# Order of the first modulation sum on VectorE, and of two side loads on the sync queue, in a hybrid decoder layer

## The chip, the core and the metric

The kernel runs on one core of a Trainium2 chip. The metric is the device time of one execution in microseconds, the median of several executions; smaller is better. Engines are named as in the profile: PE is TensorE (PEld its weight loads), DVE is VectorE, ACT is ScalarE, POOL is GpSimd, SP is the sync engine, whose queue (SPq) issues most DMAs; ACT issues some too (ACTq).

## What is computed

One decoder layer over 512 tokens of width 1024 (batch 1, depth 1). The change touches only the start: the modulation vector, the first norm, and the first projection.

```python
cond = jax.nn.silu(c)
mod = cond @ ada_w[l] + ada_b[l]
sh1, sc1, g1, sh2, sc2, g2 = jnp.split(mod[:, None, :], N_MOD, axis=-1)

u = rms_norm(x, mix_pre_g[l]) * (1.0 + sc1) + sh1
proj = u @ w_in[l]
...
x = x + g1 * rms_norm(mix, mix_post_g[l])
...
x = x + g2 * rms_norm(f, ffn_post_g[l])
```

Behind `proj` come a four-head mLSTM, a causal convolution of width 31 with a layer norm, the output projection, and a gated convolutional feed-forward block. All matrix products of the projections are made with operands that are split into a high and a low part (three matmuls for one).

## The kernel before

Channels lie on the 128 partitions for most of the kernel: the 1024 channels are `KT` = 8 blocks of 128, the 512 tokens are 4 tiles (`NT`).

**Opening.** `x` is loaded token by token (`xn`, eight pieces of 256 KB). For each of the four token tiles ScalarE and VectorE sum the squares of half the row each (L256, L257), VectorE adds them (`xs`, L265), GpSimd raises the sum to the power -1/2 (L266), and `x_turn` (L238 on) multiplies the identity with that factor on VectorE (`dg`, L240) and lets TensorE multiply `xn` with `dg` (L242): that turns the first four channel blocks of the tile and applies the norm in one go. A fifth matmul spreads the factor over the partitions (`rb`, L243). The other four blocks (`xr4` to `xr7`) are loaded already turned from a second input, `xT`, and are multiplied with `rb` later (L354).

**Modulation.** `cb` holds silu(c), spread over all partitions. `ada_sum(k, i)` (L271) is one VectorE instruction over 128x1024 elements: a piece of the modulation matrix (`ada`, 512 KB, loaded by `first_load`, L220) times `cb`, summed along the row, into a column of `part[k]`. Two such sums give scale and shift of channel block `k`; L334 and L335 make `gs` and `sh` (tile `gsk`) of them.

**The first projection** is a loop over the eight blocks `k` (L317). Each turn loads a weight block `wglu0` (512 KB, two buffers), splits it on ScalarE (L170, L324) and VectorE (L171, L339), makes the high part `uh` of the block's input on ScalarE (L341, L358, L361) and the low part `ul` on VectorE (L344, L365, L367), makes the two sums of block k + 1, and runs 24 matmuls of 128x512 into eight accumulators (L316, later L188 to L190). Each turn also issues side loads on SP: the two `ada` pieces of block k + 1 or later (two buffers, so the load waits for the sums that free one), one block of `xT` in turns 1 to 4 (L331), and in turn 1 the rest of the vectors (`vec[:, FIRST:]`, 296 KB, L328), whose first reader is L408 behind the loop.

**Order.** Within the opening `in_order` keeps VectorE, ScalarE and GpSimd in the order in which the code is written. A DMA is issued when all ahead of it on its queue are, and when its buffer is free. Behind the opening a scheduler sets the order of each engine from a plan of its own, so an edit in the opening can also exchange neighbours far behind it. There the convolution's taps (L731, 200 instructions on VectorE) fill the time between the instructions on which TensorE waits.

Of the kernel before, what the change touches and what calls it, by code (L numbers as in the profile page):

```python
# [10 lines left out]
F32 = mybir.dt.float32  # L11
F32R = mybir.dt.float32r
BF16 = mybir.dt.bfloat16
AF = mybir.ActivationFunctionType
ALU = mybir.AluOpType
PSUM = bass.MemoryType.PSUM

P = 128
D = 1024
# [33 lines left out]
def decoder_layer(ctx, tc, w_glu0, x, xT, c, adaT, vecs, w_glu, w_qko, w_v0, w_v, w_out, w_up, w_down, out):  # L53
    nc = tc.nc
    V, S, G, PE = nc.vector, nc.scalar, nc.gpsimd, nc.tensor
# [10 lines left out]
    small = ctx.enter_context(tc.tile_pool(name="small", bufs=6))  # L66
# [17 lines left out]
    def slot(name, dt=F32):  # L84
        return slots.tile([P, T], dt, tag="t", name=name)

    def mmbank(name):
        return psum.tile([P, T], F32, tag="mm", bufs=4, name=name)

    def atbank(name):  # L90
        return psum.tile([P, T], F32, tag="at", bufs=2, name=name)
# [27 lines left out]
    cb = const.tile([P, D], F32, name="cb")  # L119
# [9 lines left out]
    def vcol(name, i):  # L129
        a = VEC[name][0] + i  # L130
        return vec[:, a : a + 1]

    def vcols(name, i, n):
        a = VEC[name][0] + i
        return vec[:, a : a + n]
# [28 lines left out]
    def w_split(src, name, pool=None, tag="w", eng=None):  # L164

        n = src.shape[1]
        pool = pool or wpool
        hi = pool.tile([P, T], F32R, tag=tag, name=f"{name}h")
        lo = pool.tile([P, T], F32R, tag=tag, name=f"{name}l")
        S.activation(hi[:, :n], src, AF.Copy)  # L170
        (eng or G).tensor_tensor(out=lo[:, :n], in0=src, in1=hi[:, :n].bitcast(F32), op=ALU.subtract)  # L171
        return hi, lo
# [46 lines left out]
    first = []  # L219

    def first_load(k):

        r = raws.tile([P, 2048], F32, tag="raw", name=f"ada{k}")
        for i in range(2):
            nc.sync.dma_start(r[:, i * D : (i + 1) * D], adaT[k][:, i * D : (i + 1) * D])
        first.append(r)
# [8 lines left out]
    TURNED = KT // 2  # L235

    def x_turn(tt, xs):

        dg = slot(f"dg{tt}")[:, :P]
        V.tensor_scalar(out=dg, in0=ident, scalar1=xs[:, 1:], scalar2=None, op0=ALU.mult)  # L240
        for j in range(TURNED):
            PE.matmul(xT_ps[j][:, tt * P : (tt + 1) * P], xn[tt][j // NT][:, j % NT * P : (j % NT + 1) * P], dg, start=True, stop=True)  # L242
        PE.matmul(rb_ps[:, tt * P : (tt + 1) * P], ones, dg, start=True, stop=True)  # L243

    xT_ps = [mmbank(f"xT{j}") for j in range(TURNED)]
    rb_ps = atbank("rb")
    last = None
    for tt in range(NT):
        if tt == 2:
            bp1 = const.tile([P, KT], F32, name="bp1")  # L250
            V.tensor_scalar(out=bp1, in0=vcols("ada_b", 0, 2 * KT).rearrange("p (j two) -> p j two", two=2)[:, :, 0], scalar1=1.0, scalar2=None,
                            op0=ALU.add)
            g32 = const.tile([P, KT], F32, name="g32")
            V.tensor_scalar(out=g32, in0=vcols("mix_pre_g", 0, KT), scalar1=RD, scalar2=None, op0=ALU.mult)
        xsq = small.tile([P, 2], F32, tag="adap", name=f"xsq{tt}")
        S.activation(xjunks[0], xn[tt][0], AF.Square, accum_out=xsq[:, :1])  # L256
        V.scalar_tensor_tensor(out=xjunks[1], in0=xn[tt][1], scalar=1.0, in1=xn[tt][1], op0=ALU.mult, op1=ALU.mult, accum_out=xsq[:, 1:])  # L257
        if tt == 1:
            S.activation(cb, cps, AF.Silu)
            cspool.__exit__(None, None, None)  # L260
            cvpool.append(ctx.enter_context(tc.tile_pool(name="cvpool", bufs=2, space=PSUM)))
        if tt:
            x_turn(tt - 1, last)
        last = small.tile([P, 2], F32, tag="gsk", name=f"xs{tt}")
        V.tensor_scalar(out=last[:, :1], in0=xsq[:, :1], scalar1=xsq[:, 1:], scalar2=D * EPS, op0=ALU.add, op1=ALU.add)  # L265
        G.tensor_tensor(out=last[:, 1:], in0=last[:, :1], in1=mhalf[:, :1], op=ALU.pow)  # L266
    x_turn(NT - 1, last)
    rb = slot("rb_s")

    part = {}  # L270

    def ada_sum(k, i):
        if i == 0:
            part[k] = small.tile([P, 2], F32, tag="adap", name=f"adap{k}")
        junk = small.tile([P, D], BF16, tag="junk", bufs=1, name=f"junk{k}_{i}")
        V.scalar_tensor_tensor(out=junk, in0=first[k][:, i * D : (i + 1) * D], scalar=1.0, in1=cb, op0=ALU.mult, op1=ALU.mult,
                               accum_out=part[k][:, i : i + 1])

    for i in range(2):
        ada_sum(0, i)  # L280

    xr = [slot(f"xr{j}") for j in range(KT)]

    def x_out(j, eng):
        if eng is S:
            S.activation(xr[j], xT_ps[j], AF.Copy)
        else:
            V.tensor_copy(xr[j], xT_ps[j])

    def u_tiles(name):  # L290
        hi = upool.tile([P, KT, T], F32R, tag="uh", name=f"{name}h")
        lo = upool.tile([P, KT, T], F32R, tag="ul", name=f"{name}l")
        return hi, lo, [(hi[:, j, :], lo[:, j, :]) for j in range(KT)]

    _, _, u = u_tiles("u")
# [17 lines left out]
    def passes(wk, k, which):  # L313
        for a, b in ((0, 0), (1, 0), (0, 1)):
            for i in which:
                PE.matmul(banks0[i], blk(wk, i)[a], u[k][b], start=k == 0 and a == b, stop=False)  # L316

    for k in range(KT):
        wk = {}
        r = adas.tile([P, D], F32, tag="ada", name=f"wglu0_{k}")  # L320
        nc.sync.dma_start(r, w_glu0[k])
        if k == 0:
            w_hi = wpool.tile([P, T], F32R, tag="w", name="wglu0_0_1h")
            S.activation(w_hi, r[:, T:], AF.Copy)  # L324
        if k + 1 < KT:
            first_load(k + 1)
        if k == 1:
            nc.sync.dma_start(vec[:, FIRST:], vecs[:, FIRST:])  # L328
        if 1 <= k <= TURNED:
            j = TURNED + k - 1  # L330
            nc.sync.dma_start(xr[j], xT[j - TURNED])  # L331
        gsk = small.tile([P, 2], F32, tag="gsk", name=f"gsk{k}")
        gs, sh = gsk[:, :1], gsk[:, 1:]
        V.tensor_scalar(out=gs, in0=part[k][:, :1], scalar1=bp1[:, k : k + 1], scalar2=g32[:, k : k + 1], op0=ALU.add, op1=ALU.mult)  # L334
        V.tensor_scalar(out=sh, in0=part[k][:, 1:], scalar1=vcol("ada_b", 2 * k + 1), scalar2=None, op0=ALU.add)  # L335
        hi, lo = u[k]
        if k == 0:
            w_lo = wpool.tile([P, T], F32R, tag="w", name="wglu0_0_1l")
            V.tensor_tensor(out=w_lo, in0=r[:, T:], in1=w_hi.bitcast(F32), op=ALU.subtract)  # L339
            wk[1] = w_hi, w_lo  # L340
            S.activation(hi, xT_ps[0], AF.Identity, scale=gs, bias=sh)  # L341
            S.activation(rb, rb_ps, AF.Copy)
            V.tensor_scalar(out=xr[0], in0=xT_ps[0], scalar1=gs, scalar2=sh, op0=ALU.mult, op1=ALU.add)
            V.tensor_tensor(out=lo, in0=xr[0], in1=hi.bitcast(F32), op=ALU.subtract)  # L344
            wk[0] = w_split(r[:, :T], "wglu0_0_0", eng=V)
            for j in range(1, TURNED):
                x_out(j, S)
            for i in range(2):
                ada_sum(1, i)
            passes(wk, k, (6, 7, 4, 5))  # L350
            passes(wk, k, range(4))
            continue
        if k >= TURNED:
            V.scalar_tensor_tensor(out=xr[k], in0=xr[k], scalar=gs, in1=rb, op0=ALU.mult, op1=ALU.mult)  # L354
        for b in range(2):
            wk[b] = w_split(r[:, b * T : (b + 1) * T], f"wglu0_{k}_{b}", eng=V)
        if k < TURNED:
            S.activation(hi, xr[k], AF.Identity, scale=gs, bias=sh)  # L358
            S.activation(xr[k], xr[k], AF.Identity, scale=gs, bias=sh)
        else:  # L360
            S.activation(hi, xr[k], AF.Identity, bias=sh)  # L361
        if k + 1 < KT:
            ada_sum(k + 1, 0)
        if k < TURNED:
            V.tensor_tensor(out=lo, in0=xr[k], in1=hi.bitcast(F32), op=ALU.subtract)  # L365
        else:
            last_u = V.scalar_tensor_tensor(out=lo, in0=xr[k], scalar=sh, in1=hi.bitcast(F32), op0=ALU.add, op1=ALU.subtract)  # L367
        if k + 1 < KT:
            ada_sum(k + 1, 1)
        if k < 4:  # L370
            passes(wk, k, range(G0))
        else:
            for i, ps in enumerate(banks0):
                mm3(ps, blk(wk, i), u[k], False, k == KT - 1)
# [963 lines left out]
```

## Time and profile before

| | us |
|---|---|
| median of 3 executions (lowest, highest) | 772.42 (771.66, 773.45) |
| the profiled execution, its own time | 773.07 |
| span of that execution, first to last instruction | 771.4 |
| PE busy in the span | 758.4 (98%) |
| DVE busy | 610.1 (79%) |
| ACT busy | 403.8 (52%) |
| POOL busy | 352.2 (46%) |

The granted clock was 0.997. All times in the text are counted from the start of the span. A row of a timeline gives start, duration, engine, line, operation, output and inputs, shapes, and in brackets the idle time of that engine just before with what ended it; successive instructions of one engine are pipelined, so a row can start up to about 0.1 us before the one ahead of it ends.

### The profile page before, as it was taken

The page shows a single profiled execution, that of the slowest core. Times are in us where ns is not written, and L with a number is a line of the kernel's source. Part 1 is how long each engine was busy: PE and PEld are TensorE (multiplying, and loading weights), DVE is VectorE, ACT ScalarE, POOL GpSimd, SP SyncE. Part 2 cuts the span into 40 slices and gives each one's busy share as a digit, 9 for nine tenths or more (in the row PEclk, how much of TensorE's full clock was granted, in tenths as well). Part 3 has the DMA queues.
Part 4 walks back from the last instruction along what each step waited for, and adds up shares of the span by engine and source line. Part 5 has one row for each costly group of instructions (what it writes and reads, how often), then busy time and mean ns, then how long its engine had stood idle before and what let it go on. Part 6 is the DMA issues. An engine that isn't in the chain of part 4 may idle for free.

```text
span 771.4 us, 10631 instructions
## 1 busy us (share of the span) xinstructions
PE 758.4 (98%) x3709; PEld 637.5 (83%) x3709; DVE 610.1 (79%) x967; ACT 403.8 (52%) x761; POOL 352.2 (46%) x286
## 2 busy tenths in 40 slices
PE   7999999999999999999999999999999999999996
PEld 5788898778888888988888998888888888888885
DVE  6997999999999966756768798666556687799995
ACT  5447266776666447582253555444444444455762
POOL 2029578696798645443661456444444440000001
PEclk9999999999999999999999999999999999999998
DMA  8983214214022452434953753332233321777872
GB/s 320 377 301 132 90 55 164 82 40 151 30 84 107 153 179 105 164 110 164 366 199 126 253 197 130 130 130 88 110 117 129 130 89 62 255 271 241 298 260 109
DMA packets 36409, 125.33 MB, mean 162 GB/s; under 512 B 4194, under 2 KB 5634, under 8 KB 30468
## 3 DMA queue, kind: packets, MB, share of 16 engines
q1 hardware_dynamic: 24372, 96.17, 35.5%
q10 hardware_dynamic: 11984, 28.48, 10.6%
q8 instruction: 29, 0.48, 0.3%
q14 instruction: 24, 0.20, 0.1%
HBM read 113.22 MB, written 11.42 MB: 162 GB/s over the span
## 4 chain that ended last, share of the span: by engine, by line
PE 72%; DVE 21%; DMA 2%; ACT 2%; issue 2%; POOL 0%; ACTq 0%; DVEq 0%; POOLq 0%
PE up L189 10%; PE up L188 10%; DVE cv L731 10%; PE up L190 10%; PE p L1185 4%; PE glu L189 3%; PE glu L190 3%; PE glu L188 3%; PE p L189 3%; PE p L188 3%; PE p L190 3%; PE mixa L188 2%; PE mixa L190 2%; PE mixa L189 2%; PE mixb L189 2%; PE mixb L188 2%
## 5 line engine op out<-in xcount | busy, mean ns | idle before, releaser
L731 DVE SCALAR_TENSOR_TENSOR cv<-gt,cvw,cv 128x505 f32<-128x505 f32 (+24 forms) x200 | 137.3, 729 | 2.3 <-ACT cv L719 1.1
L685 POOL TENSOR_TENSOR ro2r<-ro2t,mhalf 128x1 f32<-128x1 f32 x1 | 0.5, 537 | 119.8 <-DVE ro2t L683 119.8
L727 POOL TENSOR_TENSOR cs<-cs,cs 128x510 f32<-128x510 f32 (+3 forms) x32 | 41.9, 1308 | 0.3
L171 POOL TENSOR_TENSOR wup_1024l<-wup,wup_1024h 128x512 fp32r<-128x512 f32 x20 | 27.4, 1372 | 31.6 <-ACT wup_1024h L170 31.6
L171 POOL TENSOR_TENSOR wup_0l<-wup,wup_0h 128x512 fp32r<-128x512 f32 x20 | 27.7, 1387 | 30.0 <-ACT wup_0h L170 30.0
L171 POOL TENSOR_TENSOR wup_1536l<-wup,wup_1536h 128x512 fp32r<-128x512 f32 x20 | 28.0, 1399 | 27.6 <-ACT wup_1536h L170 25.1
L155 DVE SCALAR_TENSOR_TENSOR junk<-ada,cb 128x1024 bf16<-128x1024 f32 x20 | 31.3, 1565 | 8.5 <-DMA ada<-in_adaT 8.4
L189 PE MATMUL up<-u2l,wup_0h 128*128 128x512 f32 (+1 forms) x100 | 36.5, 365 | 0.2 <-DVE u2l L910 0.2
L188 PE MATMUL up<-u2h,wup_0h 128*128 128x512 f32 (+1 forms) x100 | 36.5, 365 | 0.0
L188 PE MATMUL up<-u2h,wup_1024h 128*128 128x512 f32 (+1 forms) x100 | 36.4, 364 | 0.0
L190 PE MATMUL up<-u2h,wup_0l 128*128 128x512 f32 (+1 forms) x100 | 36.4, 364 | 0.0
L188 PE MATMUL up<-u2h,wup_512h 128*128 128x512 f32 (+1 forms) x100 | 36.4, 364 | 0.0
L189 PE MATMUL up<-u2l,wup_512h 128*128 128x512 f32 (+1 forms) x100 | 36.4, 364 | 0.0
L190 PE MATMUL up<-u2h,wup_512l 128*128 128x512 f32 (+1 forms) x100 | 36.4, 364 | 0.0
L188 PE MATMUL up<-u2h,wup_1536h 128*128 128x512 f32 (+1 forms) x100 | 36.4, 364 | 0.0
L189 PE MATMUL up<-u2l,wup_1536h 128*128 128x512 f32 (+1 forms) x100 | 36.4, 364 | 0.0
L190 PE MATMUL up<-u2h,wup_1536l 128*128 128x512 f32 (+1 forms) x100 | 36.4, 364 | 0.0
L190 PE MATMUL up<-u2h,wup_1024l 128*128 128x512 f32 (+1 forms) x100 | 36.4, 364 | 0.0
L189 PE MATMUL up<-u2l,wup_1024h 128*128 128x512 f32 (+1 forms) x100 | 36.3, 363 | 0.0
L171 POOL TENSOR_TENSOR wup_512l<-wup,wup_512h 128x512 fp32r<-128x512 f32 x20 | 27.7, 1383 | 14.0 <-ACT wup_512h L170 14.0
L725 ACT ACTIVATE cs<-gt,cvw 128x511 f32<-128x511 f32 (+4 forms) x40 | 27.4, 716 | 6.5 <-POOL cs L727 3.2
L170 ACT ACTIVATE wup_1024h<-wup 128x512 fp32r<-128x512 f32 x22 | 13.9, 631 | 25.1 <-PE up L189 20.4
(1072 smaller groups left out, 2667.0 us busy)
## 6 DMA issues: line engine op xcount, KB each, us to landing
wup<-in_w_up SPq DMA_DIRECT2D x22, 1024.0 KB, 6.5
wqko<-in_w_qko SPq DMA_DIRECT2D x12, 1024.0 KB, 4.8
ada<-in_adaT ACTq DMA_DIRECT2D x20, 512.0 KB, 4.6
ada<-in_adaT SPq DMA_DIRECT2D x16, 512.0 KB, 6.9
wo<-in_w_out SPq DMA_DIRECT2D x8, 1024.0 KB, 4.8
spare<-in_adaT ACTq DMA_DIRECT2D x12, 512.0 KB, 7.4
wd<-in_w_down SPq DMA_DIRECT2D x6, 768.0 KB, 6.7
g2kept<-g2d SPq DMA_DIRECT2D x11, 384.0 KB, 7.3
```

The source lines that it names most:

```text
L155: t = V.scalar_tensor_tensor(out=junk, in0=r, scalar=1.0, in1=cb, op0=ALU.mult, op1=ALU.mult, accum_out=mod[:, i : i + 1])
L170: S.activation(hi[:, :n], src, AF.Copy)
L171: (eng or G).tensor_tensor(out=lo[:, :n], in0=src, in1=hi[:, :n].bitcast(F32), op=ALU.subtract)
L188: PE.matmul(ps, a[0], b[0], start=start, stop=False)
L189: PE.matmul(ps, a[0], b[1], start=False, stop=False)
L190: PE.matmul(ps, a[1], b[0], start=False, stop=stop)
L685: G.tensor_tensor(out=r, in0=t, in1=mhalf[:, :1], op=ALU.pow)
L725: S.activation(t[:, d:], cvx[j][:, : T - d], AF.Copy, scale=w(CK - 1 - d))
L727: G.tensor_tensor(out=side[:, d:], in0=side[:, d:], in1=t[:, d:], op=ALU.add)
L731: last_tap[0] = V.scalar_tensor_tensor(out=cp[:, d:], in0=cvx[j][:, : T - d], scalar=w(CK - 1 - d), in1=cp[:, d:], op0=ALU.mult, op1=ALU.add)
L1185: PE.matmul(ps[q], x, y, start=False, stop=m == NM - 1 and i == 2, skip_group_check=True)
```

## The change

The sum over the first `ada` piece is written ahead of the last tile's `x_turn`, and so ahead of `dg3` on VectorE; the sum over the second piece stays behind it. The rest of the vectors is loaded in turn 6 of the loop and no longer in turn 1. The turned rows `xr4` to `xr7` are loaded in turns 2 to 5 and no longer in turns 1 to 4.

```diff
+    part = {}
+
+    def ada_sum(k, i):
+        if i == 0:
+            part[k] = small.tile([P, 2], F32, tag="adap", name=f"adap{k}")
+        junk = small.tile([P, D], BF16, tag="junk", bufs=1, name=f"junk{k}_{i}")
+        V.scalar_tensor_tensor(out=junk, in0=first[k][:, i * D : (i + 1) * D], scalar=1.0, in1=cb, op0=ALU.mult, op1=ALU.mult,
+                               accum_out=part[k][:, i : i + 1])
 
     xT_ps = [mmbank(f"xT{j}") for j in range(TURNED)]
...
         G.tensor_tensor(out=last[:, 1:], in0=last[:, :1], in1=mhalf[:, :1], op=ALU.pow)
+    ada_sum(0, 0)
     x_turn(NT - 1, last)
     rb = slot("rb_s")
...
-    for i in range(2):
-        ada_sum(0, i)
+    ada_sum(0, 1)
...
-        if k == 1:
+        if k == 6:
             nc.sync.dma_start(vec[:, FIRST:], vecs[:, FIRST:])
-        if 1 <= k <= TURNED:
-            j = TURNED + k - 1
+        if 2 <= k <= TURNED + 1:
+            j = TURNED + k - 2
             nc.sync.dma_start(xr[j], xT[j - TURNED])
```

On VectorE, at the end of the norm's sums, the order before was (`xs3` and `dg3` are the last tile's factor and diagonal, `junk0_0` and `junk0_1` the two sums of block 0, `gsk0` its scale and shift):

```order
L265 TENSOR_SCALAR xs3_200<-xsq3_190 128x1
L240 TENSOR_SCALAR dg3_203<-ident_93,xs3_200 128x128
L276 SCALAR_TENSOR_TENSOR junk0_0_212,adap0_211<-ada0_138,cb_112 128x1024
L276 SCALAR_TENSOR_TENSOR junk0_1_214,adap0_211<-ada0_138,cb_112 128x1024
L334 TENSOR_SCALAR gsk0_241<-adap0_211,bp1_173,g32_175 128x1
L335 TENSOR_SCALAR gsk0_241<-adap0_211,vec_111 128x1
```

and now it is:

```order
L274 TENSOR_SCALAR xs3_200<-xsq3_190 128x1
L251 SCALAR_TENSOR_TENSOR junk0_0_204,adap0_203<-ada0_138,cb_112 128x1024
L240 TENSOR_SCALAR dg3_206<-ident_93,xs3_200 128x128
L251 SCALAR_TENSOR_TENSOR junk0_1_214,adap0_203<-ada0_138,cb_112 128x1024
L334 TENSOR_SCALAR gsk0_241<-adap0_203,bp1_173,g32_175 128x1
L335 TENSOR_SCALAR gsk0_241<-adap0_203,vec_111 128x1
```

One sum and `dg3` have changed places; nothing is added.

On the sync queue, from the load of `ada2` on, the order before was:

```order
L225 DMA ada2_288<-in_adaT 128x1024 x2
L328 DMA vec_111<-in_vecs 128x592
L331 DMA xr4_220<-in_xT 128x512
L321 DMA wglu0_2_336<-in_w_glu0 128x1024
L225 DMA ada3_338<-in_adaT 128x1024 x2
L331 DMA xr5_221<-in_xT 128x512
L321 DMA wglu0_3_385<-in_w_glu0 128x1024
```

and now it is:

```order
L225 DMA ada2_288<-in_adaT 128x1024 x2
L321 DMA wglu0_2_334<-in_w_glu0 128x1024
L225 DMA ada3_336<-in_adaT 128x1024 x2
L331 DMA xr4_220<-in_xT 128x512
L321 DMA wglu0_3_383<-in_w_glu0 128x1024
L225 DMA ada4_385<-in_adaT 128x1024 x2
L331 DMA xr5_221<-in_xT 128x512
```

Ahead of `wglu0_3` the vectors and one block of `xr` are gone; the vectors now stand between `ada7` and `wglu0_7`.

TensorE's order is the same, instruction by instruction. On VectorE, ScalarE and GpSimd neighbours have changed places in the middle of the kernel. In head 0 the normed output `hn0`, which TensorE turns (L555), stands 13 VectorE instructions earlier. In head 2, where `E20` to `E22` are the weighted scores that free a bank for TensorE's next scores (L514), and `junk_21` to `junk_23` sums of later modulation columns (L155), VectorE's order before was:

```order
L515 SCALAR_TENSOR_TENSOR E20_2510<-s2_0_2720,E20_2510 128x512
L155 SCALAR_TENSOR_TENSOR junk_21_3180,mod_137<-ada_21_3178,cb_112 128x1024
L515 SCALAR_TENSOR_TENSOR E21_2511<-s2_1_2724,E21_2511 128x384
L155 SCALAR_TENSOR_TENSOR junk_22_3184,mod_137<-ada_22_3182,cb_112 128x1024
L155 SCALAR_TENSOR_TENSOR junk_23_3188,mod_137<-ada_23_3186,cb_112 128x1024
```

and now it is:

```order
L515 SCALAR_TENSOR_TENSOR E20_2510<-s2_0_2720,E20_2510 128x512
L515 SCALAR_TENSOR_TENSOR E21_2511<-s2_1_2724,E21_2511 128x384
L155 SCALAR_TENSOR_TENSOR junk_21_3180,mod_137<-ada_21_3178,cb_112 128x1024
L155 SCALAR_TENSOR_TENSOR junk_22_3184,mod_137<-ada_22_3182,cb_112 128x1024
L155 SCALAR_TENSOR_TENSOR junk_23_3188,mod_137<-ada_23_3186,cb_112 128x1024
```

`E21` no longer stands behind a modulation sum.

More of the change, by code (lines that the diff above doesn't have):

```diff
@@ L266, in decoder_layer @@
         G.tensor_tensor(out=last[:, 1:], in0=last[:, :1], in1=mhalf[:, :1], op=ALU.pow)
+    ada_sum(0, 0)
     x_turn(NT - 1, last)
     rb = slot("rb_s")
[L270 to L277, printed above, removed]
-    for i in range(2):
-        ada_sum(0, i)
+    ada_sum(0, 1)
     xr = [slot(f"xr{j}") for j in range(KT)]
```

## The prediction

> **What bounds the kernel now.** I read the busy time by stage first, then TensorE's waits over the whole span, then the chain of waits, and last the timelines of the engines around the edit. The columns of the first view are the stretch and its length, and then for each engine busy microseconds and instructions, the granted clock, the DMA share and GB/s.
>
> ```profile
> 15.76:38.00 22.24, 22.19 (x96) 18.05 (x97) 21.09 (x42) 12.31 (x20) 0.00 (x0) 1.00 1.00 372
> 60.00:300.00 240.00, 238.83 (x1195) 200.19 (x1194) 216.96 (x341) 147.77 (x292) 176.68 (x143) 1.00 0.31 105
> 300.00:765.00 465.00, 464.73 (x2283) 393.44 (x2281) 341.63 (x514) 225.20 (x416) 163.61 (x126) 1.00 0.49 172
> ```
>
> TensorE is busy for all but 0.05 us of the first, 1.17 of the second and 0.27 of the third stretch. A gain must therefore come from an earlier start of its dense work at 15.76, or out of one of the few waits behind it. These are all of them (us in total, times, longest):
>
> ```profile
> PE glu L316 <- ACT uh L341: 0.9, 1, 0.9
> PE s L514 <- DVE E L515: 0.4, 1, 0.4
> PE hT L555 <- DVE hn L549: 0.4, 1, 0.4
> PE s L514 <- DVE so L557: 0.3, 1, 0.3
> PE glu L189 <- DVE ul L367: 0.3, 1, 0.3
> PE up L189 <- DVE u2l L910: 0.2, 1, 0.2
> ```
>
> Behind the first row these sum to 1.6 us: that, and what the start gives, is all that any reordering can win. The chain of waits adds that VectorE is not a spectator:
>
> ```profile
> PE 72%; DVE 21%; DMA 2%; ACT 2%; issue 2%; POOL 0%; ACTq 0%; DVEq 0%; POOLq 0%
> ```
>
> **Term A, the start.** TensorE's first dense matmul waits for `uh` on ScalarE, which waits for `gsk` on VectorE, which waits for both sums.
>
> ```profile
> 10.96 0.21 DVE L265 TENSOR_SCALAR xs<-xsq 128x1 f32<-128x1 f32 x1
> 11.82 0.29 DVE L240 TENSOR_SCALAR dg<-ident,xs 128x128 f32<-128x128 f32 x1 [0.66 <-POOL xs L266]
> 12.02 1.22 DVE L276 SCALAR_TENSOR_TENSOR junk<-ada,cb 128x1024 bf16<-128x1024 f32 x1
> 13.17 0.09 DVE L276 DVE_READ_ACCUMULATOR junk<-ada,cb 128x1 f32 x1
> 13.29 1.22 DVE L276 SCALAR_TENSOR_TENSOR junk<-ada,cb 128x1024 bf16<-128x1024 f32 x1
> 14.44 0.27 DVE L334 TENSOR_SCALAR gsk<-adap,bp,g 128x1 f32<-128x1 f32 x1
> 14.63 0.20 DVE L335 TENSOR_SCALAR gsk<-adap,vec 128x1 f32<-128x1 f32 x1
> ```
>
> VectorE idles 0.66 us for GpSimd's factor; the moved sum goes into that hole. It cannot start before its data:
>
> ```profile
> 5.33 0.80 SPq L225 DMA_DIRECT2D ada<-in_adaT  x2
> ada<-in_adaT SPq DMA_DIRECT2D x1, 512.0 KB, 6.0
> ada<-in_adaT SPq DMA_DIRECT2D x1, 512.0 KB, 6.9
> ```
>
> The first piece lands 6.0 us after its issue at 5.33, at about 11.33, the second, issued 0.4 later, 6.9 after that issue, at 12.6. Without any collision the first sum starts at 11.33, hands over after 1.15 (12.02 to 13.17) at 12.48 to `dg`, the second starts 0.20 later (11.82 to 12.02) at 12.68, `gsk` at 13.83 and its second part at 14.02 to 14.22. ScalarE then decides:
>
> ```profile
> 13.89 0.63 ACT L324 ACTIVATE wglu_1h<-wglu 128x512 fp32r<-128x512 f32 x1 [3.79 <-DMA wglu<-in_w_glu]
> 14.93 0.78 ACT L341 ACTIVATE uh<-xT,gsk 128x512 fp32r<-128x512 f32 x1 [0.40 <-PE rb L243]
> ```
>
> It is busy with a weight split until 14.52, so `uh` could start at 14.53 and no earlier: the upper bound is 14.93 - 14.53 = 0.40. The bracket blames `rb`, but `uh` reads `xT` and not `rb`, and `gsk` ended at 14.83, 0.10 before; I read it as a wait for `gsk`.
>
> There is a collision, however. The factor for which VectorE idled is still being made:
>
> ```profile
> 9.79 0.93 POOL L266 TENSOR_TENSOR xs<-xs,mhalf 128x1 f32<-128x1 f32 x1 [1.41 <-DVE xs L265]
> 11.24 0.55 POOL L266 TENSOR_TENSOR xs<-xs,mhalf 128x1 f32<-128x1 f32 x1 [0.52 <-DVE xs L265]
> ```
>
> The one at 9.79 ran beside a VectorE instruction and took 0.38 longer than the one that ran alone. Further on, the same kind of sum as the moved one shows the other direction:
>
> ```profile
> 252.89 1.22 DVE L155 SCALAR_TENSOR_TENSOR junk<-ada,cb 128x1024 bf16<-128x1024 f32 x1
> 264.62 2.31 DVE L155 SCALAR_TENSOR_TENSOR junk<-ada,cb 128x1024 bf16<-128x1024 f32 x1
> ```
>
> ```profile
> 264.11 1.74 POOL L171 TENSOR_TENSOR wqko_1536l<-wqko,wqko_1536h 128x512 fp32r<-128x512 f32 x1
> ```
>
> GpSimd was first, until 265.85; the sum ended at 266.93, which is 1.22 after 265.71. It did nothing until GpSimd was nearly done. Here GpSimd starts at 11.24, ahead of 11.33, and ends at 11.79; taken like that row, the sum works from 11.65, hands over at 12.80, the second sum starts at 13.00, `gsk` ends at 14.54, and `uh` starts 0.10 later at 14.64: a gain of 0.29. Had it to wait to the very end of GpSimd's instruction, 0.15 less. The range of term A is 0.15 to 0.40, and I take 0.3, near the row of the same instruction.
>
> The Trainium skill's page "SBUF — State Buffer", section "Who interferes with whom", states the rule behind these rows: a VectorE instruction with two inputs in SBUF and a GpSimd instruction that reads SBUF share a port pair, and whichever starts first blocks the other for its whole length. By that rule the sum goes ahead only from 11.79 and term A is 0.15; by no contention at all it is 0.40. The trace agrees with the blocking and puts the release 0.14 ahead of the end.
>
> What `dg` loses is covered: it would end at 12.80 + 0.29 = 13.09, while TensorE reaches the last tile only here:
>
> ```profile
> 13.58 1.06 PE L242 MATMUL xT<-dg,xn 128*128 128x128 f32 x8
> 15.76 1.20 PE L316 MATMUL glu<-uh,wglu_1h 128*128 128x512 f32 x4 [0.90 <-ACT uh L341]
> ```
>
> There is 0.49 us of room. Were it gone, each delay of `dg` would delay all four turned blocks one for one.
>
> **Term B, the wait at the fifth block.**
>
> ```profile
> 21.83 0.33 SPq L321 DMA_DIRECT2D wglu<-in_w_glu  x1
> 29.81 0.63 ACT L170 ACTIVATE wglu_0h<-wglu 128x512 fp32r<-128x512 f32 x1 [2.86 <-DMA wglu<-in_w_glu]
> 30.47 0.69 DVE L171 TENSOR_TENSOR wglu_0l<-wglu,wglu_0h 128x512 fp32r<-128x512 f32 x1 [1.07 <-ACT wglu_0h L170]
> 37.90 0.74 DVE L367 SCALAR_TENSOR_TENSOR ul<-xr,gsk,uh 128x512 fp32r<-128x512 f32 x1
> 38.70 0.50 PE L189 MATMUL glu<-ul,wglu_0h 128*128 128x512 f32 x1 [0.29 <-DVE ul L367]
> ```
>
> The load of `wglu0_3` takes 8 us because the DMA engines are full (share 1.00, 372 GB/s above). VectorE loses 1.07 us on it and never gets it back before `ul` of block 4, for which TensorE waits 0.29. The change takes these out from ahead of that load:
>
> ```profile
> vec<-in_vecs SPq DMA_DIRECT2D x1, 296.0 KB, 6.9
> xr<-in_xT SPq DMA_DIRECT2D x1, 256.0 KB, 7.1
> ```
>
> 552 KB at 372 GB/s is 1.5 us. The load then lands near 28.3, its split ends 0.66 later (29.81 to 30.47) at 29.0, and VectorE, 0.3 earlier by term A, wants it at 30.47 - 1.07 - 0.3 = 29.1: no wait. `ul` ends at 38.64 - 1.07 - 0.3 = 37.3, and TensorE comes there at 38.41 - 0.3 = 38.1. Its 0.29 is gone: term B is 0.29, and at worst 0, if the loads go no faster than now. The opening gives A + B = 0.6, with 0.15 to 0.69 as bounds.
>
> The later side loads cost nothing, because of these first readers:
>
> ```profile
> 34.88 0.75 DVE L354 SCALAR_TENSOR_TENSOR xr<-xr,gsk,rb_s 128x512 f32<-128x512 f32 x1
> 52.80 1.38 DVE L408 TENSOR_SCALAR cvw<-vec 128x248 f32<-128x248 f32 x1
> ```
>
> `xr4` now goes out right behind `ada3`, where `xr5` stood, just ahead of the issue at 21.83; with 7.1 us it lands near 29, and its reader comes at 34.88 - 1.4 = 33.5. The vectors go out behind `ada7`, at about 40, and with 6.9 us land near 47, against 51.4. If the vectors came too late, VectorE would stop behind the loop's last `ul`, and no longer ahead of it.
>
> **Term C, the middle.** The scheduler's exchanges touch two of TensorE's waits.
>
> ```profile
> 202.58 1.47 PE L555 MATMUL hT<-ident,hn 128*128 128x128 f32 x8 [0.40 <-DVE hn L549]
> ```
>
> ```profile
> 269.16 1.71 DVE L155 SCALAR_TENSOR_TENSOR junk<-ada,cb 128x1024 bf16<-128x1024 f32 x1
> 270.80 0.55 DVE L515 SCALAR_TENSOR_TENSOR E<-s,E 128x384 f32<-128x384 f32 x1
> ```
>
> ```profile
> 271.40 0.49 PE L514 MATMUL s<-q_0c,k_2c 128*128 128x128 f32 x2 [0.45 <-DVE E L515]
> ```
>
> `hn0` stands 13 instructions earlier, so 0.40 should go. The second wait is for `E21`, which stood behind a modulation sum of 1.71; now the sum follows it, so 0.45 should go. That is 0.85 at most. Against it, each sum in that stretch can meet a GpSimd instruction and grow from 1.22 to 2.31, and the change deals these meetings anew; from the trace I cannot say which fall where. One such meeting, 1.09, more than eats both. I take half, 0.4; the bounds are 0.85 and, with one more meeting on the path, 0.85 - 1.09 = -0.24.
>
> **Sum.** 0.3 + 0.3 + 0.4 = 1.0 us. The profiled execution took 773.07 with a span of 771.4; it would take 772.1 with a span of 770.4. That execution lies 0.65 above the median of the three, 772.42, which becomes 771.4.
>
> **Rivals.** About 0.2%, 1.5 us, is what a measurement here can tell from no change.
>
> *All of it arrives.* No collision for the first sum (0.40), 0.29, both later waits (0.85), and the 0.3 for `so`: 1.84, so 770.6. For it: TensorE's order is untouched, and nothing else holds it. Against it: the rows of collisions.
>
> *The opening's gain is eaten in the middle.* VectorE has 21% of the chain, which in order of time runs over its convolution (`cv`, L731) in the middle of the kernel. If its work there does not come earlier, TensorE's lead of 0.6 is lost in the waits at 202 and 271, and the time stays near 772.4. Against it: ahead of that stretch VectorE still waits for what TensorE feeds.
>
> ```profile
> 93.91 0.69 DVE L389 SCALAR_TENSOR_TENSOR gt<-gt,glu 128x512 f32<-128x512 f32 x1 [0.62 <-ACT gt L387]
> ```
>
> *Slower.* Two more meetings of sum and GpSimd between 254 and 271, ahead of `so` or `E20`: 2 x 1.09 = 2.2, less the opening's 0.6, is 1.6: 774.0. It decides as soon as `E20` or `E21` ends more than 0.6 later than now. For it: VectorE and GpSimd are both busy there, and two of TensorE's three waits in the middle lie there. Against it: several sums in this stretch are already prolonged, so there are few free ones to hit.
>
> *The move does not do what it says.* If the first piece landed 0.5 later than at 11.33, the sum would hold up `dg` beyond 13.58 and term A would vanish. The landing is set by loads that do not change.
>
> **How the numbers follow.** Forecast 0.44 (771.4), all of it 0.25 (770.6), eaten 0.15 (772.4), slower 0.14 (774.0), other 0.02. Faster by over 0.2% means under 770.9: most of the second case and, by the spread of a median (the three runs lie 1.8 apart), about a fifth of the first, 0.30. Slower by over 0.2% means over 773.96: 0.14 with a little from elsewhere, and the rest, 0.56, is no change that can be told. The likeliest case alone spans 770.6 to 772.2. The range for 8 in 10 goes from 769.9 (the second case less 0.7 for the spread) to 773.3.
>
> **What would show it.** The first sum starts at about 11.3; it lasts 1.5 to 1.7 us if it meets GpSimd's instruction, 1.22 if not; `dg` ends ahead of 13.5; `uh` starts at 14.5 to 14.8 and TensorE's first dense matmul 0.15 to 0.4 ahead of 15.76. VectorE has no wait of 1 us ahead of the weight split of block 3, and TensorE none at the fifth block. TensorE's waits for `hn` and `E` are gone or stand elsewhere. I am wrong if the opening's lead is there at 60 us and the end is not earlier, or if a new wait of TensorE over 0.5 us stands between 100 and 300.

## The result, and the profile after

The changed kernel takes 776.78 us (median of 4 executions, 775.92 to 777.45) against 772.12 for the kernel before (4 executions): a ratio of 1.005, with a 95% interval of 1.0032 to 1.0068. It is slower by about 4 us (2.5 to 5.3), where 771.4 was forecast. The profiled execution took 775.92 with a span of 774.2. One execution in all the runs, the one of 1280.94 us among the eleven of opening_new_middle_old, ran at a granted clock of 0.558 and is left out of that run's ratio.

All of the loss lies behind the opening, which comes out ahead. In the timeline of the changed kernel, VectorE, then GpSimd, then TensorE:

```profile
10.21 0.21 DVE L274 TENSOR_SCALAR xs<-xsq 128x1 f32<-128x1 f32 x1
11.30 1.23 DVE L251 SCALAR_TENSOR_TENSOR junk<-ada,cb 128x1024 bf16<-128x1024 f32 x1 [0.87 <-DMA ada<-in_adaT]
12.45 0.28 DVE L240 TENSOR_SCALAR dg<-ident,xs 128x128 f32<-128x128 f32 x1
13.81 0.27 DVE L334 TENSOR_SCALAR gsk<-adap,bp,g 128x1 f32<-128x1 f32 x1
```

```profile
15.22 1.21 PE L316 MATMUL glu<-uh,wglu_1h 128*128 128x512 f32 x4 [0.24 <-ACT uh L341]
```

The sum starts at 11.30 and isn't prolonged, `dg` ends at 12.73, and the dense work starts 0.54 ahead of 15.76. But note `xs` at 10.21: in the profile before it stood at 10.96, so this execution was ahead before the edit could act.

TensorE's waits over the whole span of the changed kernel (us in total, times, longest):

```profile
PE s L514 <- DVE so L557: 3.2, 2, 2.0
...
PE aT L626 <- DVE ga L621: 0.4, 1, 0.4
PE glu L316 <- ACT uh L341: 0.2, 1, 0.2
PE up L189 <- DVE u2l L910: 0.2, 1, 0.2
```

The waits for `E`, `hn` and `ul` are gone, as term C and term B said. In their place the wait for `so` (the gated output of a head, which VectorE makes at L557 and for which TensorE's next scores wait), 0.3 before, is 3.2 in two pieces: 2.00 in head 0 and 1.25 in head 2. The timeline of VectorE shows how the first piece comes about, and GpSimd's shows beside what:

```profile
193.77 4.25 DVE L549 TENSOR_SCALAR hn<-hn,fac 128x256 f32<-128x256 f32 x4
197.94 1.37 DVE L731 SCALAR_TENSOR_TENSOR cv<-gt,cvw,cv 128x504 f32<-128x504 f32 x2
199.22 0.68 DVE L602 TENSOR_TENSOR Md<-Mb,cmask 128x512 f32<-128x512 f32 x1
199.82 7.12 DVE L731 SCALAR_TENSOR_TENSOR cv<-gt,cvw,cv 128x503 f32<-128x503 f32 x11
206.85 0.68 DVE L557 SCALAR_TENSOR_TENSOR so<-so,hT 128x512 f32<-128x512 f32 x1
```

```profile
193.89 1.37 POOL L171 TENSOR_TENSOR wqko_0l<-wqko,wqko_0h 128x512 fp32r<-128x512 f32 x1
195.22 1.33 POOL L727 TENSOR_TENSOR cs<-cs,cs 128x509 f32<-128x509 f32 x1
196.52 1.34 POOL L749 TENSOR_TENSOR ysq<-ysq,ydl 128x512 f32<-128x512 f32 x1
197.83 1.34 POOL L171 TENSOR_TENSOR wqko_512l<-wqko,wqko_512h 128x512 fp32r<-128x512 f32 x1
```

The four `hn` multiplications of head 0, in their new place 13 instructions earlier, take 4.25 us. In the profile before, in the old place, they took 1.13, and GpSimd's last instruction had ended at 200.75:

```profile
193.19 1.30 POOL L727 TENSOR_TENSOR cs<-cs,cs 128x509 f32<-128x509 f32 x1
...
195.84 1.30 POOL L727 TENSOR_TENSOR cs<-cs,cs 128x508 f32<-128x508 f32 x1
197.08 1.30 POOL L171 TENSOR_TENSOR wqko_512l<-wqko,wqko_512h 128x512 fp32r<-128x512 f32 x1
...
199.72 1.03 POOL L546 TENSOR_TENSOR fac<-ssq,mhalf 128x4 f32<-128x4 f32 x1
```

```profile
202.09 1.13 DVE L549 TENSOR_SCALAR hn<-hn,fac 128x256 f32<-128x256 f32 x4
```

On TensorE the changed kernel then shows this (the turned `hT` first, then the scores that wait for `so`, then the next projection):

```profile
201.43 1.29 PE L555 MATMUL hT<-ident,hn 128*128 128x128 f32 x8
...
207.58 1.74 PE L514 MATMUL s<-q_0c,k_2c 128*128 128x512 f32 x2 [2.00 <-DVE so L557]
209.12 1.91 PE L514 MATMUL s<-q_1c,k_3c 128*128 128x512 f32 x2
...
212.10 0.69 PE L188 MATMUL qko<-uh,wqko_0h 128*128 128x512 f32 x1
```

`hT` was done near 202.7, but VectorE came to `so` only at 206.85. And the matmuls behind the wait are slow, 1.74 and 1.91 where before two such took 1.02. The windows say why; the column ahead of the last two is the granted clock:

```profile
205.00:210.00 5.00, 3.00 (x9) 1.38 (x9) 5.00 (x10) 2.44 (x5) 1.72 (x2) 0.80 0.01 2
210.00:215.00 5.00, 5.00 (x18) 3.37 (x17) 5.00 (x8) 3.95 (x8) 5.00 (x5) 0.86 0.34 105
```

So a suspicion stands for the first piece: GpSimd held up `hn`, VectorE (busy without a gap from there to `so`) passed the 3.1 us on to `so`, and the clock fell on top. A trace shows coincidence; the runs below try it.

The second piece has something else ahead of it as well. Just ahead of that `so` VectorE stood idle for a load of `ada` and then made a sum that was itself prolonged:

```profile
262.09 2.12 DVE L155 SCALAR_TENSOR_TENSOR junk<-ada,cb 128x1024 bf16<-128x1024 f32 x1 [1.59 <-DMA ada<-in_adaT]
```

```profile
264.87 1.13 PE L514 MATMUL s<-q_0c,k_2c 128*128 128x512 f32 x2 [1.25 <-DVE so L557]
```

The profile before has nearly the same idle time (1.57) and the same sum (2.13) there, with a wait of 0.33. How much of this piece the new order makes isn't shown.

### The profile page after: what moved, and what is told of

Its sections match the earlier page's. It is cut to its first block, busy times and chain, and to the rows that moved or that the text cites. A ratio compares the mean times of both kernels' runs of the same rounds, so it can differ in the third digit from the quotient of the medians.

```text
span 774.2 us, 10635 instructions
## 1 busy us (share of the span) xinstructions
PE 759.9 (98%) x3709; PEld 638.8 (83%) x3709; DVE 614.8 (79%) x967; ACT 403.0 (52%) x761; POOL 351.7 (45%) x286
## 4 chain that ended last, share of the span: by engine, by line
PE 76%; DVE 16%; ACT 3%; DMA 2%; issue 1%; POOL 0%; SPq 0%; ACTq 0%; DVEq 0%; POOLq 0%
PE up L189 10%; PE up L190 10%; PE up L188 10%; DVE cv L731 9%; PE p L1185 4%; PE glu L316 3%; PE glu L190 3%; PE glu L188 3%; PE glu L189 3%; PE p L189 3%; PE p L190 3%; PE p L188 3%; PE mixa L188 2%; PE mixa L190 2%; PE mixa L189 2%; PE mixb L189 2%
## 5 line engine op out<-in xcount | busy, mean ns | idle before, releaser
L731 DVE SCALAR_TENSOR_TENSOR cv<-gt,cvw,cv 128x502 f32<-128x502 f32 (+24 forms) x200 | 137.3, 730 | 3.2 <-ACT cv L719 2.1
L155 DVE SCALAR_TENSOR_TENSOR junk<-ada,cb 128x1024 bf16<-128x1024 f32 x20 | 30.9, 1548 | 9.5 <-DMA ada<-in_adaT 9.4
L171 POOL TENSOR_TENSOR wup_512l<-wup,wup_512h 128x512 fp32r<-128x512 f32 x20 | 27.6, 1382 | 14.6 <-ACT wup_512h L170 14.6
```

The source lines that it names most:

```text
L155: t = V.scalar_tensor_tensor(out=junk, in0=r, scalar=1.0, in1=cb, op0=ALU.mult, op1=ALU.mult, accum_out=mod[:, i : i + 1])
L731: last_tap[0] = V.scalar_tensor_tensor(out=cp[:, d:], in0=cvx[j][:, : T - d], scalar=w(CK - 1 - d), in1=cp[:, d:], op0=ALU.mult, op1=ALU.add)
```

## The experiments

Behind the opening both kernels have the same instructions; only their order on VectorE, ScalarE and GpSimd differs, from about 55 to 280 us. Most experiments therefore force an order with a table of instruction numbers, each one tied behind the one ahead of it on its engine without any wait. The table moves the lines of those kernels: L589 there is L549 here, L597 is L557 (40 more).

```diff
+    placed = {i.name: i for i in nc.cur_bb.bb.instructions}
+    for ids in ORDER:
+        ids = [f"I-{n}" for n in ids.split()]
+        for a, b in zip(ids, ids[1:]):
+            tc.add_manual_dep(placed[b], a, mybir.DependencyInfo(mybir.DependencyClass.NoSync, mybir.DependencyReason.DATA),
+                              reason="order by table")
```

All runs, each against the kernel before on the same chip (its medians there: 771.81, 772.08 and 772.15 us for the three groups of rows):

| run | median, us | ratio to before, 95% interval |
|---|---|---|
| opening_new_middle_old | 771.52 | 0.9995 (0.9986 to 1.0004) |
| opening_old_middle_new | 776.34 | 1.0058 (1.0046 to 1.0070) |
| head0_old_order | 774.82 | 1.0039 (1.0026 to 1.0053) |
| hn0_back_alone | 772.85 | 1.0011 (1.0001 to 1.0021) |
| sum_alone | 771.88 | 0.9997 (0.9988 to 1.0005) |
| gpsimd_held | 772.88 | 1.0007 (0.9997 to 1.0017) |
| so_earlier | 779.24 | 1.0090 (1.0070 to 1.0110) |
| hn0_on_scalar | 772.14 | 0.9999 (0.9989 to 1.0009) |
| loads_alone | 776.58 | 1.0055 (1.0040 to 1.0070) |
| loads_alone_old_order | 772.37 | 1.0004 (0.9996 to 1.0013) |
| three_waits_removed | 770.71 | 0.9981 (0.9972 to 0.9989) |

### Opening against middle

The edit above and no other: the changed code with a table of the old order for all three engines, and the old code with a table of the new one.

> The changed opening, but behind it VectorE, ScalarE and GpSimd follow the order of the kernel before, instruction by instruction. Theory O (the loss is made by the order in the middle alone): the 1.1 us that the changed kernel was ahead at 55 us come through, less what TensorE again waits for hn (0.4) and E (0.45) as it did before; about 771.0 to 771.6, a ratio of 0.998 to 0.9995. Rival L (the moved sum or the late loads cost it by themselves): 775 to 777, with a wait of TensorE over 1 us between 200 and 270. Rival S (the loss is spread, half of it from each): about 774.

> The opening of the kernel before, but behind it the order that the changed kernel has on VectorE, ScalarE and GpSimd. Theory O: slower than the changed kernel by what its opening gains, 777 to 778, ratio 1.006 to 1.0075, and VectorE's four hn instructions of head 0 take over 3 us. Rival L: 772.0 to 772.6, ratio 1.000. Rival S: about 774.5.

Measured 771.52 and 776.34. The loss goes with the order of the middle and not with the opening's code: rival L and rival S fall. What the new opening gives by itself is 0.3 us, with an interval of -0.3 to 1.1 (0.9986 to 1.0004 of 771.8). In the second run the four `hn` of head 0 behave as in the changed kernel; the first row is a tile's view (count, shortest/median/longest in ns) of the run with the new order, the second of the run with the old:

```profile
L589 DVE TENSOR_SCALAR hn<-hn,fac x4: 345/1382/1391, 194.0 to 196.9; 128x256 f32<-128x256 f32 x4
```

```profile
L589 DVE TENSOR_SCALAR hn<-hn,fac x4: 339/340/340, 200.3 to 201.1; 128x256 f32<-128x256 f32 x4
```

One ran at 345 ns and three at about 1382, 1.04 us more each: these three make the 3.1 us.

### Which half of the change turns the order over

The two halves of the change each alone, without any table; and the loads once more with the old order forced.

```diff
-        if k == 6:
+        if k == 1:
             nc.sync.dma_start(vec[:, FIRST:], vecs[:, FIRST:])
-        if 2 <= k <= TURNED + 1:
-            j = TURNED + k - 2
+        if 1 <= k <= TURNED:
+            j = TURNED + k - 1
```

(That is sum_alone, as an edit of the changed kernel; loads_alone is the kernel before with the opposite edit.)

> Only the moved sum; the loads stand as before. Without any table the scheduler then gives behind the opening the same order as in the kernel before, so no order is forced here. Theory O with term A as predicted: 0.2 to 0.5 us faster than before, ratio 0.9993 to 0.9998, and TensorE's first dense matmul comes 4.2 to 4.6 us after the last xs of VectorE, in place of 4.8 (15.76 - 10.96); the time of opening_new_middle_old, 771.5, should be nearly reached. If the later loads carried the gain (term B): 771.8 to 772.1, with the wait for ul at the fifth block back. If the sum itself costs: over 772.5.

> Only the later loads; the sum stands as before, and no order is forced. The scheduler then gives behind the opening the very order that the changed kernel has there, hn0 13 places earlier among it. Theory O with the blocking: all of the loss, like opening_old_middle_new, ratio 1.0045 to 1.007, 775.5 to 777.5, and the four hn of head 0 take over 4 us. If the loss needed the moved sum too: 772 to 773.

> Only the later loads, with the order of the kernel before forced behind the opening on VectorE, ScalarE and GpSimd. This is term B alone. If the wait at the fifth block (0.29) is there in every execution of the kernel before: 771.5 to 771.9, 0.2 to 0.4 below before. If that wait was a matter of the one profiled execution: within 0.2 of before, ratio 0.9997 to 1.0003. If the later loads cost something by themselves: 772.5 and more.

The built orders say it already: the moved sum leaves the middle exactly as it was, and the later loads give exactly the order of the changed kernel. The times follow: 0.9997 for the sum, 1.0055 for the loads, 1.0004 for the loads with the old order. The loads cost nothing as loads; they cost 4 us by the order that the scheduler makes when they stand later. Term B isn't there: with the old order the later loads give between 0.3 us gained and 1.0 lost.

### The four `hn` instructions alone

In the changed kernel, nothing is moved but these rows of VectorE:

```diff
 L731 SCALAR_TENSOR_TENSOR cv5<-gt5,cvw,cv5
-L549 TENSOR_SCALAR hn0<-hn0,fac0 (four of them)
 L731 SCALAR_TENSOR_TENSOR cv6<-gt6,cvw,cv6
...
 L731 SCALAR_TENSOR_TENSOR cv6<-gt6,cvw,cv6
+L549 TENSOR_SCALAR hn0<-hn0,fac0 (four of them)
 L731 SCALAR_TENSOR_TENSOR cv5<-gt5,cvw,cv5
```

> The changed kernel, with only the four hn instructions of head 0 on VectorE put back, by 13 places, to just ahead of the last two taps before so. Theory O with the blocking of hn by GpSimd as its cause: the four take 1.1 to 1.5 us in place of 4.2, so comes 2.5 to 3 us earlier, and the time is 772 to 774. If it is not the blocking but the later places of Md and the taps, or GpSimd's and ScalarE's exchanges: 775.5 to 777, with the wait for so still over 1 us.

772.85: of the 0.50% the changed kernel loses, 0.11% are left. `hn` ran free (339 to 340 ns each), the wait for `so` in head 0 is gone, and the granted clock is 1.00 there. One sign of the other reading came true all the same: a wait for `so` of over 1 us, 1.46 in head 2. VectorE idled 2.14 us for a load of `ada` ahead of it, so this second wait doesn't need the blocking of `hn`. The time speaks for `hn`, but not yet for GpSimd: the instructions behind `hn` changed places too. So the next run leaves every instruction of the changed kernel where it is and only makes GpSimd stand still while `hn` runs.

```diff
+    tc.add_manual_dep(placed["I-2189"], "I-1978", mybir.DependencyInfo(mybir.DependencyClass.Sync, mybir.DependencyReason.DATA), reason="GpSimd held")
```

> The changed kernel, all orders as they are, with one wait added: GpSimd's weight split wqko_0l of head 2 waits until the last hn instruction of head 0 is done, so that GpSimd stands still while hn runs in its early place. Theory blocking (hn is held up by GpSimd's instructions, three of 1.33 us): the four hn take 1.1 to 1.5 us in place of 4.2, the waits for so shrink as in hn0_back_alone, 772.3 to 774. Theory place (it is the position of hn and the taps behind it, not the meeting with GpSimd): 775.5 to 777. GpSimd loses 1.2 us there and has 2.6 us to spare at 200 us.

772.88, by a wait that was added. VectorE's and GpSimd's timelines in that run:

```profile
193.87 1.13 DVE L589 TENSOR_SCALAR hn<-hn,fac 128x256 f32<-128x256 f32 x4
194.92 1.37 DVE L771 SCALAR_TENSOR_TENSOR cv<-gt,cvw,cv 128x504 f32<-128x504 f32 x2
196.20 0.68 DVE L642 TENSOR_TENSOR Md<-Mb,cmask 128x512 f32<-128x512 f32 x1
196.80 7.12 DVE L771 SCALAR_TENSOR_TENSOR cv<-gt,cvw,cv 128x503 f32<-128x503 f32 x11
203.83 0.67 DVE L597 SCALAR_TENSOR_TENSOR so<-so,hT 128x512 f32<-128x512 f32 x1
```

```profile
195.23 1.30 POOL L211 TENSOR_TENSOR wqko_0l<-wqko,wqko_0h 128x512 fp32r<-128x512 f32 x1 [1.20 <-DVE hn L589]
```

```profile
PE s L554 <- DVE so L597: 0.7, 1, 0.7
```

At the same place (193.87 against 193.77) the four take 1.13 us in place of 4.25, `so` comes at 203.83 in place of 206.85, and TensorE's wait for `so` falls from 3.2 to 0.7, all of it in head 2; between 200 and 215 us the granted clock is 1.00. The eleven taps take 7.12 us in both runs, though here GpSimd is at work again from 195.23. That is the cause of the first wait and of the slow matmuls behind it, shown: the meeting with GpSimd, and not the place as such. The Trainium skill's page "SBUF — State Buffer", section "Who interferes with whom", names copies, casts and `tensor_scalar` among the VectorE operations that can take the port pair shared with GpSimd, and says that an instruction with at most one input in SBUF, outside such a mode, doesn't contend. The rows agree on both: `hn` is held up, the taps, whose accumulator `cv` lies in PSUM, aren't.

The third way to part the two is to take `hn` from VectorE altogether.

```diff
-            V.tensor_scalar(out=hv, in0=hv, scalar1=fac[:, tt : tt + 1], scalar2=None, op0=ALU.mult)
+            if h == 0:
+                S.activation(hv, hv, AF.Copy, scale=fac[:, tt : tt + 1])
+            else:
+                V.tensor_scalar(out=hv, in0=hv, scalar1=fac[:, tt : tt + 1], scalar2=None, op0=ALU.mult)
```

> The changed kernel, with the four hn multiplications of head 0 on ScalarE (behind the second weight split of wqko2_1) and not on VectorE, all else in order. Theory blocking: ScalarE isn't held up by GpSimd, its four take 1.2 to 1.8 us; VectorE gains all 4.2 us; both waits for so are under 0.5 us; 771.3 to 772.8. If the order of the other instructions costs: over 775.

772.14, the level of the kernel before. On ScalarE, while GpSimd works, the four take

```profile
193.60 1.70 ACT L590 ACTIVATE hn<-hn,fac 128x256 f32<-128x256 f32 x4
```

### What didn't help

The changed kernel, with `so` and `hl` of head 0 six taps earlier on VectorE:

```diff
 L731 SCALAR_TENSOR_TENSOR cv (five taps)
+L557 so0, tap, L557 so1, two taps, L561 hl0, tap, L561 hl1
 L731 SCALAR_TENSOR_TENSOR cv (six taps)
-L557 so0, tap, L557 so1, two taps, L561 hl0, tap, L561 hl1
 L515 SCALAR_TENSOR_TENSOR E10
```

> The changed kernel, with so and hl of head 0 six taps earlier on VectorE, right where hT is ready; hn stays in its early place and is still blocked for 3 us. Theory lost time (VectorE is loaded to the full from 160 to 260 us, so the 3 us come back at the next place where TensorE waits for it): the first wait for so goes, and with it the slow matmuls, but the one near 263 us grows from 1.2 to 2 to 3.5; 774.5 to 776.5. Theory place (only so standing behind eleven taps costs): 772.5 to 773.5, second wait unchanged.

779.24, worse than the changed kernel. The first wait for `so` is gone and the second one has all of it, as the theory of lost time said, but larger than expected:

```profile
PE s L554 <- DVE so L597: 4.3, 1, 4.3
```

Behind that wait the granted clock was 0.56 (265 to 270 us). Moving the victim does not give back the 3 us that VectorE lost. Six taps now stand ahead of `E10`, VectorE idled 0.80 for a load of `ada` just ahead of this `so`, and this execution also started 0.8 later than the changed kernel's (16.03 against 15.22); what each adds to the 4.3 isn't shown.

The changed kernel, with head 0's stretch of the table in the old order:

```diff
-L546 TENSOR_TENSOR fac0<-ssq0,mhalf
 L727 TENSOR_TENSOR cs5_1<-cs5_1,cs5_2
...
 L727 TENSOR_TENSOR cs5_1<-cs5_1,cs5_5
+L546 TENSOR_TENSOR fac0<-ssq0,mhalf
```

(This is GpSimd's largest move in it; VectorE's is the one of `hn0`.)

> The changed kernel, with only head 0's stretch put back in the old order: 42 instructions of VectorE, 24 of ScalarE and 13 of GpSimd, around 190 to 215 us. Theory O in its narrow form (that stretch holds nearly all of the loss: waits for so of 2.0 and 1.2 us, and 1.6 us of slow matmuls behind the first): 771.3 to 772.5. If the loss is spread over the middle's exchanges: 774 to 776. Rival L: 776 to 777.

774.82, in the range of a spread loss, but by another mechanism. `hn` ran free there, yet a new wait stood ahead of it:

```profile
188.80 1.77 DVE L785 SCALAR_TENSOR_TENSOR ydl<-ysum,gt 128x512 f32<-128x512 f32 x1 [1.47 <-POOL gt L779]
...
203.33 1.12 DVE L589 TENSOR_SCALAR hn<-hn,fac 128x256 f32<-128x256 f32 x4
```

```profile
PE hT L595 <- DVE hn L589: 2.5, 1, 2.5
```

In the new order the last tap of `cv4` comes two places later on VectorE, and in the old order of head 0 ScalarE turns to its result first of all. The seam between two good pieces made a stall that neither has. A stretch of an order can't be judged by cutting it out.

### A version that beats both

The changed opening and the old order, with three exchanges: `hn0` two taps earlier (behind GpSimd's last instruction still), so one tap earlier, `E21` ahead of the modulation sum `junk_21`.

```diff
+L549 TENSOR_SCALAR hn0<-hn0,fac0 (four of them)
 L731 SCALAR_TENSOR_TENSOR cv5, cv6 (two taps)
-L549 TENSOR_SCALAR hn0<-hn0,fac0 (four of them)
 L731 SCALAR_TENSOR_TENSOR cv5
+L557 SCALAR_TENSOR_TENSOR so0
 L731 SCALAR_TENSOR_TENSOR cv6
-L557 SCALAR_TENSOR_TENSOR so0
...
+L515 SCALAR_TENSOR_TENSOR E21
 L155 SCALAR_TENSOR_TENSOR junk_21
-L515 SCALAR_TENSOR_TENSOR E21
```

> The changed opening and the old order behind it, with three exchanges on VectorE: hn0 two taps earlier (still behind GpSimd's factor, which ends at 200.75 in the profile of before, and with GpSimd idle), so one tap earlier, and E21 ahead of the modulation sum junk_21. Theory O: the waits for hn (0.3) and E (0.4) of opening_new_middle_old go: 770.6 to 771.3, ratio 0.998 to 0.9993. If other waits take their place at once: 771.3 to 772.

770.71 us (median of 11, 769.94 to 771.21), a ratio of 0.9981 (0.9972 to 0.9989): faster than the kernel before by 0.8 to 2.2 us. TensorE's waits behind the opening's first loads are down to these:

```profile
PE p L229 <- DVE t_4l L1054: 0.3, 1, 0.3
PE s L554 <- DVE E L555: 0.2, 1, 0.2
PE up L229 <- DVE u2l L950: 0.2, 1, 0.2
```

## Why the prediction was wrong, point by point

**What bounds the kernel: right, for gains only.** The list of TensorE's waits bounds what a reordering can win; three_waits_removed won about what it allowed. It says nothing of what a reordering can lose, and I took it as if it did.

**Term A (0.3): not resolved in the time.** sum_alone gives 0.2 us, between 0.9 gained and 0.4 lost. Two of its steps were off. First, the collision with GpSimd's factor didn't come as forecast. In opening_new_middle_old GpSimd starts 0.05 ahead, and the sum takes its free time:

```profile
10.70 0.55 POOL L315 TENSOR_TENSOR xs<-xs,mhalf 128x1 f32<-128x1 f32 x1 [0.52 <-DVE xs L314]
```

```profile
10.75 1.23 DVE L291 SCALAR_TENSOR_TENSOR junk<-ada,cb 128x1024 bf16<-128x1024 f32 x1
```

In so_earlier the sum was 0.06 ahead, and it was GpSimd that was held up, 1.57 in place of 0.55; `dg` then waited for it until 13.37, where it could have started at 12.85, behind the sum:

```profile
11.70 1.23 DVE L291 SCALAR_TENSOR_TENSOR junk<-ada,cb 128x1024 bf16<-128x1024 f32 x1
```

```profile
11.76 1.57 POOL L315 TENSOR_TENSOR xs<-xs,mhalf 128x1 f32<-128x1 f32 x1 [0.52 <-DVE xs L314]
```

So the moved sum can delay the very factor in whose time it was to run. The prediction shows a factor prolonged by 0.38 beside a VectorE instruction, but prices the other direction alone.

Second, "the landing is set by loads that do not change" is true of the load and not of the race that decides. In loads_alone, with the old order of the opening, the norm was early, and the first sum started behind `dg` at the time at which its data came in the changed kernel (11.30):

```profile
10.24 0.21 DVE L265 TENSOR_SCALAR xs<-xsq 128x1 f32<-128x1 f32 x1
...
11.31 1.23 DVE L276 SCALAR_TENSOR_TENSOR junk<-ada,cb 128x1024 bf16<-128x1024 f32 x1
```

```profile
15.23 1.20 PE L316 MATMUL glu<-uh,wglu_1h 128*128 128x512 f32 x4 [1.12 <-ACT uh L341]
```

With `xs` at the same time as in the changed kernel's profile (10.21), the dense work starts at the same time (15.22) without the moved sum. The move pays only in executions in which the norm is the late one. In the profiles in which the last `xs` starts at 10.41 or later, the dense work starts 4.79 to 4.81 behind it without the moved sum and 4.26 to 4.65 with it; where `xs` starts at 10.21 to 10.26, it is 4.99 without it and 4.97 to 5.01 with it.

**Term B (0.29): not there.** The wait for `ul` stood in the one profiled execution of before. opening_old_middle_new has the same opening and no such wait among TensorE's, and loads_alone_old_order shows no gain. I took a wait of one execution for a wait of the kernel.

**Term C (0.4, bounds -0.24 to 0.85): this step failed.** "`hn0` stands 13 instructions earlier, so 0.40 should go": both waits did go, and the earlier place cost 3.1 us. (The 0.45 for `E21` was worth less than that: in opening_old_middle_new, gpsimd_held and hn0_on_scalar, with the same order there, TensorE waits 0.30 to 0.36 for `E20` instead.) I priced the meetings of GpSimd with the modulation sums alone, because I had a row for that, and took the moved `TENSOR_SCALAR` at its old duration. The profile of before had what was needed. Thirteen places of some 0.65 (twelve taps and `Md`) are 8.4 us; 202.1 less 8.4 is near 194, and GpSimd's instructions of before, of which some are quoted above, stand without a gap from there to 200.75.

**What the price grew into.** The changed kernel's span is 4.8 us longer than that of opening_new_middle_old, which differs in the order alone. More waits: 3.2 for `so` and 0.4 for `ga`, less the 0.3 for `hn` and 0.4 for `E` that the other run has, 2.9. Slow matmuls: from the first score to the next projection 4.52 us (207.58 to 212.10), where that run takes 2.71:

```profile
205.00 1.02 PE L554 MATMUL s<-q_0c,k_2c 128*128 128x512 f32 x2
...
207.71 0.69 PE L228 MATMUL qko<-uh,wqko_0h 128*128 128x512 f32 x1
```

That is 1.8 more. And 0.55 of that run's earlier start (14.67), which is no effect of the order. Together 5.25; 4.8 of it arrived at the end, and where the rest was caught up I haven't traced. Of the waits, the 2.0 in head 0 is traced to `hn`; the 1.25 in head 2 is not.

**The rivals.** "Slower" had the right mechanism, a VectorE instruction held up by GpSimd on the way to `so`, with a chance of 0.14; it had the wrong instruction and place (sums between 254 and 271) and no price for the clock, so 774.0 in place of 776.8. "Eaten in the middle" asked whether VectorE's lead comes through, and not whether its order stays good. The two signs named at the end, a lead at 60 us that is lost by the end and a new wait of over 0.5 us between 100 and 300, are what the profile showed.

## What to carry to other kernels

When an edit lets a scheduler exchange instructions far away, price each exchanged instruction at its new place: which engine runs beside it there, and does that engine hold it up; a duration from the old place is no price. Where an engine has no gap between a delayed instruction and the next one that others wait for, a delay of 3 us isn't absorbed but handed on, and here moving the waiting instruction only moved the wait; hold the blocker, or move the blocked one to where the blocker is idle. A wait or a lead of some tenths in one profiled execution can be that execution's DMA landings: look for it in a second profile before it becomes a term.

## What the hardware showed

The clock falls after some waits of TensorE and not after others of the same length. In the changed kernel the wait of 2.00 us for `so` was followed by slow matmuls, in loads_alone one of 2.01 at the same place wasn't; there the clock fell after a later wait for `so`, of 2.4 (windows of loads_alone, the granted clock ahead of the last two columns):

```profile
205.00:210.00 5.00, 2.99 (x12) 1.65 (x11) 5.00 (x10) 2.40 (x5) 1.73 (x2) 1.00 0.00 0
265.00:270.00 5.00, 5.00 (x13) 2.55 (x12) 4.86 (x4) 2.38 (x5) 5.00 (x4) 0.74 0.59 191
```

In head0_old_order a wait of 2.48 cost no clock at all. The Trainium skill's page "TensorE: Matmul & The Clock Gate", section "What's actually happening", gives a window of about 3.4 us that runs freely, and at least one idle window as the condition for the lower clock. That the outcome differs from run to run fits a free-running window; that 2.0 us of waiting were enough twice (in the changed kernel and in opening_old_middle_new, granted clock 0.80 and 0.79 from 205 to 210 us) doesn't fit the figure.

GpSimd's 128x1 power of 0.55 us didn't hold up a two-input sum that started 0.05 behind it (1.23 us), but such a sum that started 0.06 ahead of the power prolonged it to 1.57 us. GpSimd's 128x512 operations held up three of the four `hn` by 1.04 us each.
